# The mixing product and the FFN's first block in 1024-column blocks, with a seam by token halves

## The chip, the cores and the metric

One core of one Trainium2 chip runs the whole kernel. The metric is the device time in microseconds; the time before is the median of three runs, 1722.13 us (1721.88 to 1722.79). In the profile PE is TensorE (matmuls and transposes), DVE is VectorE, ACT is ScalarE, POOL is GpSimd, and SP issues most of the DMAs.

## The reference

One layer of a hybrid decoder block on 256 tokens of width 2048: attention and a gated recurrence run side by side, are joined by two gates, and a SwiGLU FFN follows. What matters here is its end:

```python
y = jax.nn.sigmoid(gate_a) * (attn @ w_attn_branch[layer]) + jax.nn.sigmoid(gate_r) * (r_out @ w_hgrn_branch[layer])
h = h + rmsnorm(y @ w_mix_out[layer], norm_mix_post[layer])
a = rmsnorm(h, norm_ffn_pre[layer])
gt, up = jnp.split(a @ w_ffn_gate_up[layer], [D_FF], axis=-1)
ff = (jax.nn.silu(gt) * up) @ w_ffn_down[layer]
h = h + rmsnorm(ff, norm_ffn_post[layer])
```

The mixing product is `y @ w_mix_out` (2048 x 2048). The first RMS norm needs all its columns before one column of h is known, and h's own norm is applied behind the gate and up products, as a factor per token (`r2c`).

## The kernel before

**Products.** Each float32 operand is split into a high and a low part, and a product is three matmuls: high by high, high by low, low by high. ACT makes the high part of a weight tile (`w` from `raw`), DVE the low part (`wl`). Activations are stationary, 128 tokens at a time (a *side*, or token half), and weights are streamed 512 columns at a time into PSUM banks. There are two kinds of blocks:

- An "N" block (`Block`) makes 512 output columns. Its steps, called chunks, take two 128-row slices of the depth each: 12 matmuls, into two banks.
- A wide block (`Wide`) makes two groups of 512 columns. A plain step takes a pair m of slices, for two sides and two groups: eight products, 24 matmuls, into four banks. A step marked `(m, 1)` in the block's order does the 2 x 2 x 2 of sides, groups and slices with seven products instead of eight: 21 matmuls. For that DVE and ACT form four combinations of the weights (`sum`, then `w`, `wl`) beside the parts of three of its raw groups (`dh`, `dl`), and four combinations of the activations of that pair (`pair_sums`, tiles `f`, `s`, `so`). Seven banks are open then, and `gather` and an evacuation put them together.

PSUM has two pools of four banks, `acc` and `aux`; a block's four banks are in one, its three extra ones in the other, by `flip`. Transposes take banks of either.

**What sets the order.** A list of items (chunks and steps) is walked in order. For each item `prepare(i)` splits the weights of item i + 2 and asks SP for the loads ahead (three `raw` buffers, three `w` buffers), `multiply` issues the matmuls, and then the *lanes* advance: generators for side work (norms, pair sums, transposes), which are taken one stage per step. `flush` empties such a queue on the spot. Every engine takes its instructions in the order in which this loop writes them.

**Around the change.** The items are, in order: two gate blocks, four blocks of the recurrent branch, four of the attention branch (all N blocks), four N blocks of `w_mix_out`, two N blocks for the FFN's first 512 gate and up columns, ten wide blocks (`GATE_UP`) for the others, and the down product. `evac_attn_branch` makes y, whose transposes (`turned`, tile `yT`) run into the first mixing block. `evac_mix` squares and scales each mixing block as it ends; gains and x (`gpost`, `hx`) are loaded on the ACT queue at the first. `begin_ffn` opens the FFN: six matmuls on a zero tile (`keep_warm`), the transposes of h's first pair into `hT`, and the next residuals; `more_h` brings the other pairs, one per step, and later starts the pair sums of `hT`; `second_norm` sums the squares for `r2c`. The first block's result u is transposed (`turn_act`) after the second step of the next block. Lines of before that the prediction's rows carry: L118 matmuls, L296/L297 the split of a chunk, L342/L344 of a plain step, L348 to L362 of a seven-product step, L434 to L454 pair sums, L509 and L522 transposes, L529/L533 hT, L1048 to L1086 the mixing's end, L1132 second norm, L1184/L1190 gate and u.

Of the kernel before, what the change touches and what calls it, by code (L numbers as in the profile page):

```python
# [20 lines left out]
P = 128  # L21
# [41 lines left out]
class Wide:  # L63
# [7 lines left out]
    def __init__(self, w, cols, order, xs, seven, evac, flip, prep=None, pre=None, mid=None,  # L71
                 turn=None, halves=False):
        self.w, self.cols, self.order, self.xs, self.seven = w, cols, order, xs, seven
        self.evac, self.flip, self.prep, self.pre, self.mid = evac, flip, prep, pre, mid
        self.turn, self.halves, self.post = turn, halves, None
        self.last7 = max((i for i, (m, s) in enumerate(order) if s), default=None)
        self.bank, self.open, self.rest = {}, set(), None


@with_exitstack  # L80
def tile_hybrid_block(ctx: ExitStack, tc: tile.TileContext, t, out):
# [251 lines left out]
    def split_wide(n):  # L333
# [3 lines left out]
        prep = b.prep(m, by7) if b.prep else iter(())  # L337
        next(prep, None)
        hi, lo = wslot(), p3("wl", F32R, 2048, 3)
        if not by7:  # L340
# [105 lines left out]

    x7 = {}

    def pair_sums(src, out, slot):

        for m in H7:
            f = ptile("f").rearrange("p (k t) -> p k t", k=2)
            x = src.slots[m]
            nc.vector.tensor_add(f, x[:, :, 0, :].bitcast(F32), x[:, :, 1, :].bitcast(F32))  # L454
# [318 lines left out]
    def fetch_gates():  # L773
        for j in range(2):
            gates["r", j] = nslot("gate")
            fetch(gates["r", j], ("r", j), "(b p) c -> p b c", p=P)
        for j in range(4):
            gates["a", j] = hslot("gate")
            fetch(gates["a", j], ("a", j), "(b p) c -> p b c", p=P)
# [204 lines left out]

    def evac_gate(key, slot):
        def go(banks):
            d = gates[key] = slot("gate")
            if d.ndim == 2:
                d = gates[key] = d.rearrange("p (b c) -> p b c", b=2)
            for i in range(2):  # L990
# [9 lines left out]
    def evac_rec_branch(j):  # L1000
        def go(banks):
            part[j] = nslot("part")
            for i in range(2):
# [4 lines left out]
    def evac_attn_branch(j):  # L1008
        def go(banks):
            if not yT:  # L1010
                yT.append(Split("yT", KD))
            y = nslot("y")
            for i in range(2):
                nc.vector.tensor_mul(y[:, i, :], banks[i], gates["a", j][:, i, :])
                nc.vector.tensor_add(y[:, i, :], y[:, i, :], part[j][:, i, :])
                yield
# [6 lines left out]

    def begin_mix():
        nc.scalar.preload_act_table_set("natural_log_exp_and_others")
        zss.append(small("zss"))

    def mix_loads():
        for j in range(2):
            gpost.append(fslot("gpost"))  # L1030
            nc.scalar.dma_start(
# [3 lines left out]
        for j in range(4):  # L1035
            hx[j] = fslot("hx").rearrange("p (b c) -> p b c", b=2)
            nc.scalar.dma_start(hx[j], xv[:, :, j * 512 : (j + 1) * 512])

    def evac_mix(j):
        def go(banks):  # L1040
            if j == 0:
                mix_loads()
            zg[j] = fslot("zg").rearrange("p (b c) -> p b c", b=2)
            for i in range(2):
                ps = banks[i]
                junk = ptile("junk")
                sq = zss[0][:, 4 * i + j : 4 * i + j + 1]
                nc.scalar.activation(junk, ps, AF.Square, accum_out=sq)  # L1048
                if j == 3:
                    rsqrt_mean(rzc[:, i : i + 1], sq, D, zss[1][i])  # L1050
                    residual(0, 0, 128, (i,), False)
                    residual(0, 128, 256, (i,), False)
                else:
                    post_gain(j, i, ps)
                yield
            if j == 2:
                zss.append(so_far(zss[0]))
        return go

    def post_gain(j, i, ps):  # L1060
        nc.vector.tensor_mul(
            zg[j][:, i, :], ps, gpost[j // 2][:, (j % 2) * 512 : (j % 2 + 1) * 512]
        )

    def so_far(ss):

        b = small("base")
        nc.vector.tensor_reduce(
            b[:, :2], ss.rearrange("p (b j) -> p b j", b=2)[:, :, :3], op=OP.add,
            axis=mybir.AxisListType.X,  # L1070
        )
        nc.vector.tensor_scalar(b[:, :2], b[:, :2], 1.0 / D, EPS, op0=OP.mult, op1=OP.add)
        nc.vector.tensor_scalar(b[:, 2:4], b[:, :2], -0.5, None, op0=OP.mult)
        return [(b[:, i : i + 1], b[:, 2 + i : 3 + i]) for i in range(2)]

# [13 lines left out]

    def begin_ffn():  # L1090
        keep_warm(BRIDGE)
        flush(evacs)
        hT.append(Split("hT", KD))
        high, low = transpose_in(h_t, colg[:, 16:32], hT[0], 0, True)
        for kk in range(2):
            high(kk)
            low(kk)
        residual_of(1, False)
        residual_of(2, False)

    def residual_of(m, spread=True):

        residual(m // 2, m % 2 * 256, m % 2 * 256 + 256, spread=spread)

    def mid_ffn():
        transpose_in(h_t, colg[:, 16:32], hT[0], 1)
        residual_of(3)
        lanes[0].append(second_norm())

    def more_h(c):  # L1110
        if c + 2 < KD // 2:
            transpose_in(h_t, colg[:, 16:32], hT[0], c + 2)
        if c + 4 < KD // 2:
            residual_of(c + 4)
        if c < 2:
            post_gain(3, c, blocks[last_mix].banks[c])
        if c == 5:
            end_phase1()
        if c == 6:
            lanes[1].append(  # L1120
                pair_sums(
                    hT[0], h7,
                    lambda: p3("so", F32R, 1024, 4),
                )
            )

# [22 lines left out]

    act_t, gate_t, h7 = [], {}, {}  # L1150

# [20 lines left out]

    def evac_first_gate(banks):
        g = gate_t[0] = [eslot("g") for _ in range(2)]
        src = banks
        if "r2" not in ready:
            for i in range(2):
                nc.scalar.activation(g[i], banks[i], AF.Copy)
                yield
            src = g  # L1180
            while "r2" not in ready:
                yield
        for i in range(2):
            nc.scalar.activation(g[i], src[i], AF.Silu, scale=r2c[:, i : i + 1])  # L1184
            yield

    def evac_first_up(banks):
        u = [eslot("u") for _ in range(2)]
        for i in range(2):
            nc.vector.scalar_tensor_tensor(  # L1190
                out=u[i], in0=banks[i], scalar=r2c[:, i : i + 1], in1=gate_t[0][i],
                op0=OP.mult, op1=OP.mult,
            )
        turns.append(u)
        yield

# [127 lines left out]
    def begin_wides():  # L1324
        flush(evacs)
        flush(lanes[1])

    early = [
        ("g", "g", COL_GR, 512),
        (("a", 0), ("a", 1), COL_GA, 512),  # L1330
        (("a", 2), ("a", 3), COL_GA + 1024, 512),
        (("r", 0), ("r", 1), COL_GB, 512),
    ]
# [23 lines left out]
    for j in range(2, 4):  # L1357
        add("N", w_in, KD, COL_GB + 512 * j, xT, evac_gate(("r", j), fslot))
    for j in range(4):
        add("N", t["w_hgrn_branch"][0], 8, 512 * j, lambda k: recT[0](k), evac_rec_branch(j),  # L1360
            pre=begin_branches if j == 0 else None)
    for j in range(4):
        add("N", t["w_attn_branch"][0], 8, 512 * j, lambda k: attnT[0](k), evac_attn_branch(j),
            pre=flush_lanes if j == 0 else None)
    for j in range(4):
        add("N", t["w_mix_out"][0], KD, 512 * j, lambda k: yT[0].after(turns)(k), evac_mix(j),
            pre=begin_mix if j == 0 else None)
    last_mix = len(blocks) - 1
    w = t["w_ffn_gate_up"][0]
    add("N", w, KD, 0, lambda k: hT[0](k), evac_first_gate,  # L1370
        pre=begin_ffn, mid=mid_ffn, post=more_h)
    add("N", w, KD, FF, lambda k: hT[0](k), evac_first_up)
    for j in range(1, 11):
# [20 lines left out]
    for i in range(len(items)):  # L1394
# [7 lines left out]
        if not wide and n in items_pre:  # L1402
            items_pre[n]()
        if not (wide and b.mid):
            prepare(i)
# [82 lines left out]
```

## Time and profile before

| | |
|---|---|
| median of three runs | 1722.13 us |
| profiled execution | 1722.56 us, span 1720.8 us |
| granted clock of TensorE, mean | 0.998 |
| busy: PE, DVE, ACT | 1703.5, 1358.7, 898.7 us |
| mixing product, first to last matmul | 914.79 to 1003.30 us |
| FFN's first block | up to 1053.66 us, where the first `GATE_UP` step starts |

A row of a timeline gives the start, the duration, the engine, the line, the operation, its tiles and how many instructions it merges; in brackets stands the idle time before it and what ended that. A row of the windows gives, after its length, the busy time and number of instructions of PE, weight loads, DVE, ACT and POOL, then the clock that TensorE was granted, the DMA share and GB/s. A row of the groups gives busy time and the mean of one in ns, and the idle time of its engine ahead of it. Matmuls are pipelined: one of 512 columns is shown with 0.39 us, while the next starts sooner.

### The profile page before, as it was taken

The numbers are of one execution on the slowest core, as the hardware profiler recorded it, in microseconds if no ns is written. First come the engines' busy times: TensorE is split into PE (matmuls) and PEld (weight loads), VectorE is DVE, ScalarE is ACT, GpSimd is POOL, SyncE is SP. The second block draws the span as 40 slices with busy tenths as digits, with TensorE's granted clock in tenths as the row PEclk, the third lists the DMA queues.
The fourth block names the chain that finished last, engine by engine and source line by source line (L and its number), as shares of the span: only waits on it lengthen the run. The fifth ranks groups of instructions, "written<-read, shape, count | busy, mean of one in ns | idle before, by whom it ended". The sixth has DMA issues, their size and how long they took to land.

```text
span 1720.8 us, 21495 instructions
## 1 busy us (share of the span) xinstructions
PE 1703.5 (99%) x8356; PEld 1429.9 (83%) x8357; DVE 1358.7 (79%) x1486; ACT 898.7 (52%) x1016; POOL 6.5 (0%) x16
## 2 busy tenths in 40 slices
PE   9999999999999999999999999999999999999997
PEld 7788888888888888888888878888888888888886
DVE  6888888866787877774566578888888888898997
ACT  6455555544434434445444466555555555665663
POOL 0000000000000000000000000000000000000000
PEclk9999999999999999999999999999999999999999
DMA  8466666655544545475456745555556555656663
GB/s 289 162 237 241 232 221 220 229 189 194 172 159 160 197 135 163 155 254 187 159 172 204 245 163 196 196 197 200 201 202 202 201 202 197 221 191 215 201 197 114
DMA packets 207189, 338.48 MB, mean 197 GB/s; under 512 B 10688, under 2 KB 77424, under 8 KB 207088
## 3 DMA queue, kind: packets, MB, share of 16 engines
q1 hardware_dynamic: 201360, 325.71, 56.9%
q10 hardware_dynamic: 5728, 11.41, 1.8%
q8 instruction: 65, 1.06, 0.3%
q14 instruction: 36, 0.29, 0.1%
HBM read 328.69 MB, written 8.39 MB: 196 GB/s over the span
## 4 chain that ended last, share of the span: by engine, by line
PE 89%; DVE 6%; issue 2%; ACT 2%; DMA 1%; ACTq 0%; DVEq 0%; SPq 0%
PE acc L118 61%; PE aux L118 26%; DVE wl L344 1%; DVE wl L360 1%; DVE dl L362 1%; DVE sum L348 1%; ACT w L356 1%; ACT w L342 0%; PE aux L522 0%; DVE sum L355 0%; DVE sum L354 0%; PE aux L840 0%; DMA gpost<-in_norm_mix_post 0%; DMA raw<-in_w_ffn_gate_up 0%; PE aux L1166 0%
## 5 line engine op out<-in xcount | busy, mean ns | idle before, releaser
L297 DVE TENSOR_TENSOR w<-raw,w 128x1024 fp32r<-128x1024 f32 x224 | 274.1, 1224 | 194.9 <-ACT w L296 193.1
L296 ACT ACTIVATE w<-raw 128x1024 fp32r<-128x1024 f32 x224 | 237.0, 1058 | 292.8 <-PE acc L118 263.0
L118 PE MATMUL acc<-xT,w 128*128 128x256 f32 (+1 forms) x2048 | 366.6, 338 | 0.0
L118 PEld LDWEIGHTS acc<-xT,w 128*128 128x128 f32 x2048 | 311.6, 188 | 44.0
L344 DVE TENSOR_TENSOR wl<-raw,w 128x2048 fp32r<-128x2048 f32 (+1 forms) x131 | 284.1, 2173 | 48.7 <-ACT w L342 46.4
L342 ACT ACTIVATE w<-raw 128x2048 fp32r<-128x2048 f32 (+1 forms) x131 | 237.7, 1819 | 103.1 <-PE acc L118 34.9
L360 DVE TENSOR_TENSOR wl<-sum,w 128x2048 fp32r<-128x2048 f32 x63 | 144.3, 2291 | 57.4 <-ACT w L356 57.4
L118 PE MATMUL acc<-w,hT 128*128 128x512 f32 x622 | 183.1, 391 | 0.3 <-ACT hT L529 0.3
L118 PE MATMUL acc<-w,xT 128*128 128x512 f32 x578 | 169.4, 392 | 0.0
L353 ACT ACTIVATE w<-sum 128x1024 fp32r<-128x1024 f32 x63 | 67.0, 1063 | 195.6 <-DVE sum L348 195.6
L118 PE MATMUL aux<-w,hT 128*128 128x512 f32 x430 | 137.3, 389 | 0.0
L118 PEld LDWEIGHTS acc<-w,hT 128*128 128x128 f32 x622 | 116.1, 188 | 24.5 <-ACT hT L529 0.5
L118 PEld LDWEIGHTS acc<-w,xT 128*128 128x128 f32 x578 | 108.1, 188 | 22.2
L362 DVE TENSOR_TENSOR dl<-raw,dh 128x1536 fp32r<-128x1536 f32 x63 | 110.4, 1752 | 0.0
L118 PE MATMUL aux<-w,xT 128*128 128x512 f32 x344 | 109.8, 389 | 0.0
L359 ACT ACTIVATE dh<-raw 128x1536 fp32r<-128x1536 f32 x63 | 93.2, 1479 | 6.6 <-PE aux L118 3.4
L118 PEld LDWEIGHTS aux<-w,hT 128*128 128x128 f32 x430 | 80.7, 188 | 16.8
L118 PE MATMUL acc<-w,yT 128*128 128x512 f32 x384 | 88.2, 390 | 0.1
L118 PEld LDWEIGHTS acc<-w,yT 128*128 128x128 f32 x384 | 71.8, 188 | 15.3 <-DVE w L297 0.5
L118 PE MATMUL acc<-w,a 128*128 128x512 f32 x268 | 83.7, 389 | 0.5 <-DVE e L1200 0.5
L118 PE MATMUL aux<-w,a 128*128 128x512 f32 x268 | 83.7, 389 | 0.0
L118 PE MATMUL aux<-wl,hT 128*128 128x512 f32 x215 | 83.6, 389 | 0.0
(262 smaller groups left out, 2624.2 us busy)
## 6 DMA issues: line engine op xcount, KB each, us to landing
raw<-in_w_in SPq DMA_DIRECT2D x270, 512.0 KB, 4.6
raw<-in_w_ffn_gate_up SPq DMA_DIRECT2D x176, 512.0 KB, 4.6
raw<-in_w_ffn_down SPq DMA_DIRECT2D x88, 512.0 KB, 4.8
raw<-in_w_mix_out SPq DMA_DIRECT2D x32, 512.0 KB, 4.9
raw<-in_w_hgrn_branch SPq DMA_DIRECT2D x16, 512.0 KB, 4.6
raw<-in_w_attn_branch SPq DMA_DIRECT2D x16, 512.0 KB, 4.5
waits<-e ACTq DMA_DIRECT2D x24, 256.0 KB, 2.6
v<-waits SPq DMA_DIRECT2D x6, 512.0 KB, 7.0
```

The lines of the kernel that those rows point to most:

```text
L118: nc.tensor.matmul(ps, lhsT, rhs, start=start, stop=stop, skip_group_check=True)
L296: nc.scalar.activation(wh, raw, AF.Copy)
L297: nc.vector.tensor_sub(wl, raw, wh.bitcast(F32))
L342: nc.scalar.activation(hi[:, c], raw[:, c], AF.Copy)
L344: nc.vector.tensor_sub(lo[:, c], raw[:, c], hi[:, c].bitcast(F32))
L348: nc.vector.tensor_sub(s[:, :1024].rearrange("p (a c) -> p a c", a=2), raw[:, 512:1536].rearrange("p (a c) -> p a c", a=2), raw[:, None, : ...
L353: nc.scalar.activation(hi[:, :1024], s[:, :1024], AF.Copy)
L356: nc.scalar.activation(hi[:, 1024:], s[:, 1024:], AF.Copy)
L359: nc.scalar.activation(dhi, d, AF.Copy)
L360: nc.vector.tensor_sub(lo, s, hi.bitcast(F32))
L362: nc.vector.tensor_sub(dlo, d, dhi.bitcast(F32))
```

## The change

- The mixing product becomes two wide blocks of 1024 columns, in orders `MIX`, with the pairs 0 and 1 by seven products: four of 16 steps. Their activation sums come from `pair_sums` on `yT` (`more_y`), and the blocks are evacuated like the down product (`mix_sum`, `mix_square`, `mix_gain`).
- The FFN's first block becomes one wide block of plain steps over the first 512 gate and up columns.
- The last two mixing steps and the first three FFN steps are written out in `mix_to_ffn` by token halves: both steps' matmuls of one side and one group, then the other; the first half's norm, residual and transposes (`turn_side`) stand between them. One of the FFN steps keeps its split weights in buffers of its own (`spare`, `Joined`). `begin_ffn` with its six matmuls on the zero tile is gone.
- The pair sums of `hT` start at step 5 of the eight and `second_norm` at step 4; `begin_wides` empties both lanes before the first `GATE_UP` step.
- The pools of the first phase are closed in the first attention-branch block (`make_room`), y is written over the attention gate, and gains, x and the branch parts use other buffers. Of the eight gate blocks, the two computed last are now those of the attention branch instead of the recurrent one.

```diff
+MIX = [
+    [(3, 0), (4, 0), (0, 1), (5, 0), (1, 1), (2, 0), (6, 0), (7, 0)],
+    [(2, 0), (3, 0), (0, 1), (4, 0), (1, 1), (5, 0), (6, 0), (7, 0)],
+]
...
+        if (b, i) == spare:
+            hi = p3("spare", F32R, 2048, 1, "sum")
+            lo = Joined(p3("spare", F32R, 1536, 1, "dh"), p3("spare", F32R, 512, 1, "dl"))
+            nc.scalar.activation(hi, raw, AF.Copy)
+            for c in (slice(0, 1536), slice(1536, 2048)):
+                nc.vector.tensor_sub(lo[:, c], raw[:, c], hi[:, c].bitcast(F32))
...
+    def mix_to_ffn(i):
...
+        prepare(i)
+        mix(0, 0)
+        base = third(0)
+        mix(0, 1)
+        norm(0, base)
+        residual(0, 0, 256, (0,), False)
+        prepare(i + 1)
+        mix(1, 0)
+        base = third(1)
+        residual(0, 256, 512, (0,), False)
+        mix(1, 1, (0,))
+        hT.append(Split("hT", KD))
+        turn_side(0, 0)
+        mix(1, 1, (1,))
+        norm(1, base)
+        turn_side(1, 0)
+        residual_of(2, (0,), False)
+        prepare(i + 2)
+        ffn(0, 0)
+        turn_side(2, 0)
+        residual(0, 0, 256, (1,), False)
+        ffn(1, 0)
+        turn_side(0, 1)
...
     def more_h(c):
...
+        if c + 1 < KD // 2:
+            transpose_in(h_t, colg[:, 16:32], hT[0], c + 1)
...
+        if c == 4:
+            residual_of(6)
+            residual_of(7)
+            lanes[0].append(second_norm())
         if c == 5:
...
+            lanes[1].append(pair_sums(hT[0], h7, lambda: p3("so", F32R, 1024, 4)))
...
     def begin_wides():
-        flush(evacs)
-        flush(lanes[1])
+        for lane in lanes:
+            flush(lane)
...
+    for j in range(2):
+        last_mix = len(wides)
+        add_wide_block(t["w_mix_out"][0], (1024 * j, 1024 * j + 512), MIX[j],
+                       lambda k: yT[0].after(turns)(k), lambda m: y7[m], evac_mix, j == 0,
+                       pre=begin_mix if j == 0 else None)
...
+    add_wide_block(w, (0, FF), PLAIN, lambda k: hT[0](k), None, evac_first, True, mid=more_h)
```

How the order moves on the engines, at three places. On PE at the seam, before: the last zero-tile matmul, the transposes of h's first 256 columns and the first FFN matmuls (`h` is the residual, `hT` its transpose, `w` a split weight).

```order
L118 LDWEIGHTS warm
L118 MATMUL aux_7945<-warm 128x512
L522 MATMUL aux_7986<-ident,h_7963 128x128 x2
L522 MATMUL aux_7989<-ident,h_7963 128x128 x2
L118 MATMUL acc_8007<-w_7912,hT_7978 128x512 x6
L522 MATMUL aux_8015<-ident,h_7963 128x128 x4
L118 MATMUL acc_8008<-w_7912,hT_7978 128x512 x6
```

On PE at the seam, now: the end of the mixing's last bank (on `yT`), two pairs of transposes of the first token half, and the first FFN matmuls.

```order
L1110 MATMUL aux_8017<-ident,h_7971 128x128 x2
L135 MATMUL aux_7728<-w_7889,yT_7114 128x512
L135 MATMUL aux_7728<-wl_7890,yT_7114 128x512
L135 MATMUL aux_7728<-w_7889,yT_7114 128x512 x2
L135 MATMUL aux_7728<-wl_7890,yT_7114 128x512
L135 MATMUL aux_7728<-w_7889,yT_7114 128x512
L1110 MATMUL aux_8041<-ident,h_7971 128x128 x2
L135 MATMUL acc_8057<-w_7920,hT_8009 128x512
```

The zero-tile matmuls are gone, and six matmuls of the mixing stand between the two pairs of transposes. On DVE the rows that lead to the second of these pairs are now: the first half's factor (`rzc`) and h, the spare split, the next bank's sum and gain, and h's second 256 columns.

```order
L153 SCALAR_TENSOR_TENSOR rzc<-a_7965,y_7964 128x1
L1097 SCALAR_TENSOR_TENSOR h_7971<-zg_7737,rzc,hx_7386 128x256
L361 TENSOR_TENSOR spare_7974<-raw_7856,spare_7973 128x1536
L361 TENSOR_TENSOR spare_7975<-raw_7856,spare_7973 128x512
L1063 TENSOR_TENSOR e_7883<-aux_7721,e_7883 128x512
L1072 TENSOR_TENSOR zg_7942<-e_7883,gpost_7384 128x512
L1339 TENSOR_REDUCE base_7998<-zss_7381 128x1
L1342 TENSOR_SCALAR base_7998<-base_7998 128x1
L1343 TENSOR_SCALAR base_7998<-base_7998 128x1
L1097 SCALAR_TENSOR_TENSOR h_7971<-zg_7737,rzc,hx_7386 128x256
```

Before, at this place DVE had the factor and two pieces of h per side, and no split:

```order
L132 SCALAR_TENSOR_TENSOR a_7957<-y_7956,v_7955 128x1
L136 SCALAR_TENSOR_TENSOR rzc<-a_7957,y_7956 128x1
L1086 SCALAR_TENSOR_TENSOR h_7963<-zg_7538,rzc,hx_7530 128x128 x2
L130 TENSOR_SCALAR v_7968<-zss_7352,base_7860 128x1
L132 SCALAR_TENSOR_TENSOR a_7970<-y_7969,v_7968 128x1
L136 SCALAR_TENSOR_TENSOR rzc<-a_7970,y_7969 128x1
L1086 SCALAR_TENSOR_TENSOR h_7963<-zg_7538,rzc,hx_7530 128x128 x2
```

The split of a weight tile and the sum of another bank have come between the factor and the columns that PE transposes. On DVE at the first `GATE_UP` steps, before: the two u, the last pair sum, and the first seven-product split.

```order
L1190 SCALAR_TENSOR_TENSOR u_8421<-acc_8264,r2c,g_8278 128x512
L1190 SCALAR_TENSOR_TENSOR u_8422<-acc_8265,r2c,g_8279 128x512
L441 TENSOR_TENSOR so_8396<-s_8416,so_8396 128x512
L348 TENSOR_TENSOR sum_8429<-raw_8343 128x1024
L354 TENSOR_TENSOR sum_8429<-raw_8343,sum_8429 128x512
L355 TENSOR_TENSOR sum_8429<-raw_8343,sum_8429 128x512
L360 TENSOR_TENSOR wl_8428<-sum_8429,w_8427 128x2048
L362 TENSOR_TENSOR dl_8436<-raw_8343,dh_8435 128x1536
```

The same place on DVE now:

```order
L466 TENSOR_TENSOR so_8456<-s_8457,so_8456 128x512
L373 TENSOR_TENSOR sum_8466<-raw_8318 128x1024
L379 TENSOR_TENSOR sum_8466<-raw_8318,sum_8466 128x512
L380 TENSOR_TENSOR sum_8466<-raw_8318,sum_8466 128x512
L385 TENSOR_TENSOR wl_8465<-sum_8466,w_8464 128x2048
L387 TENSOR_TENSOR dl_8473<-raw_8318,dh_8472 128x1536
L1256 SCALAR_TENSOR_TENSOR u_8448<-acc_8064,r2c,g_8446 128x512
L1256 SCALAR_TENSOR_TENSOR u_8449<-acc_8138,r2c,g_8447 128x512
```

The two u have moved from ahead of the split to behind it.

More of the change, by code (lines that the diff above doesn't have):

```diff
@@ L1035, in mix_loads @@
         for j in range(4):
-            hx[j] = fslot("hx").rearrange("p (b c) -> p b c", b=2)
+            hx[j] = rslot("hx").bitcast(F32).rearrange("p (b c) -> p b c", b=2)
             nc.scalar.dma_start(hx[j], xv[:, :, j * 512 : (j + 1) * 512])
[L1039 to L1058, printed above, removed]
@@ L1065, in so_far @@
[L1065 to L1074, printed above, removed]
+            zg[j][:, i, :], b.rest[i, j % 2],
```

201 lines of the change are left out of this document (127 added, 74 removed).

## Prediction

> **What bounds the kernel now.** I read the page's busy shares first, then a table of windows around the change, then the timelines of PE, ACT and DVE there.
>
> ```profile
> PE 1703.5 (99%) x8356; PEld 1429.9 (83%) x8357; DVE 1358.7 (79%) x1486; ACT 898.7 (52%) x1016; POOL 6.5 (0%) x16
> ```
> ```profile
> 915.00:1003.00 88.00, 87.95 (x392) 72.38 (x391) 47.44 (x48) 40.87 (x51) 0.00 (x0) 1.00 0.68 227
> 1003.00:1006.50 3.50, 2.42 (x12) 1.02 (x11) 2.33 (x11) 2.04 (x8) 0.00 (x0) 1.00 0.63 193
> ```
> ```profile
> 902.60 0.60 PE L509 MATMUL aux<-ident,y 128*128 128x128 f32 x4
> ...
> 914.79 8.43 PE L118 MATMUL acc<-w,yT 128*128 128x512 f32 x36
> ...
> 926.63 76.82 PE L118 MATMUL acc<-w,yT 128*128 128x512 f32 x336
> 1003.30 1.47 PE L118 MATMUL aux<-warm 128*128 128x512 bf16 x5
> 1004.60 0.27 PE L522 MATMUL aux<-ident,h 128*128 128x128 f32 x1
> ...
> 1006.52 1.71 PE L118 MATMUL acc<-w,hT 128*128 128x512 f32 x6 [0.30 <-ACT hT L529]
> ...
> 1013.22 0.60 PE L522 MATMUL aux<-ident,h 128*128 128x128 f32 x4
> 1013.57 2.99 PE L118 MATMUL acc<-w,hT 128*128 128x512 f32 x12
> ...
> 1026.01 0.60 PE L522 MATMUL aux<-ident,h 128*128 128x128 f32 x4
> ...
> 1053.66 0.39 PE L118 MATMUL aux<-w,hT 128*128 128x512 f32 x1
> ...
> 1070.19 0.39 PE L118 MATMUL aux<-w,hT 128*128 128x512 f32 x1
> ...
> 1075.63 0.39 PE L118 MATMUL acc<-w,so 128*128 128x512 f32 x1
> ```
>
> TensorE is busy all the time. In the mixing product (914.79 to 1003.30) it never waits to speak of, and DVE and ACT are busy for half of it. Only the 3.5 us of the seam to the FFN show a hole. So what the change removes on PE counts in full, and so does each new wait on PE; the question is whether DVE and ACT, which get more work in shorter bursts, still keep ahead. Two prices on PE: a plain eight-product step is 24 matmuls from 1070.19 to 1075.63, 0.227 us each; four transposes cost 0.35 (1013.22 to 1013.57).
>
> **What is saved on PE.** Four of 16 mixing steps go from 24 matmuls to 21: 12 x 0.227 = 2.7 us. The six warm-up matmuls go: 1003.30 to 1004.60, 1.3 us. From there to the first FFN matmul are 1.92 us, of which four transposes are 0.35: 1.6 us of waiting go. Together 5.6 us. The FFN block keeps its 192 matmuls, and the transposes keep their number.
>
> **What it costs: six waits.** The orders of the change put elementwise work in front of what PE wants next. I lay the rows of before end to end in the new order. Durations:
>
> ```profile
> L342 ACT ACTIVATE w<-raw 128x2048 fp32r<-128x2048 f32 x117 | 223.4, 1910 | 99.8 <-PE acc L118 34.9 <-PE aux L118 24.7 <-issue 23.9
> ```
> ```profile
> L297 DVE TENSOR_TENSOR w<-raw,w 128x1024 fp32r<-128x1024 f32 x224 | 274.1, 1224 | 194.9 <-ACT w L296 193.1
> L1015 DVE TENSOR_TENSOR y<-y,part 128x512 f32<-128x512 f32 x8 | 5.5, 692 | 0.3
> L1086 DVE SCALAR_TENSOR_TENSOR h<-zg,rzc,hx 128x256 f32<-128x256 f32 x9 | 4.8, 563 | 0.0
> ```
> ```profile
> 1033.00 0.15 DVE L602 TENSOR_REDUCE s<-ss 128x2 f32<-128x8 f32 x1
> ...
> 1034.14 0.16 DVE L136 SCALAR_TENSOR_TENSOR r2c<-a,y 128x2 f32<-128x2 f32 x1
> ...
> 1052.69 0.68 DVE L454 TENSOR_TENSOR f<-hT 128x512 f32<-128x512 f32 x1
> 1053.29 2.28 DVE L344 TENSOR_TENSOR wl<-raw,w 128x2048 fp32r<-128x2048 f32 x1
> 1055.49 0.28 DVE L434 SCALAR_TENSOR_TENSOR s<-f 128x128 f32<-128x128 f32 x1
> ...
> 1056.42 1.41 DVE L1190 SCALAR_TENSOR_TENSOR u<-acc,r2c,g 128x512 f32<-128x512 f32 x2
> 1057.74 0.68 DVE L441 TENSOR_TENSOR so<-s,so 128x512 fp32r<-128x512 f32 x1
> 1058.34 1.22 DVE L348 TENSOR_TENSOR sum<-raw 128x1024 f32<-128x1024 f32 x1
> ...
> 1066.02 2.28 DVE L344 TENSOR_TENSOR wl<-raw,w 128x2048 fp32r<-128x2048 f32 x1
> ```
> ```profile
> 1003.49 0.60 ACT L1048 ACTIVATE junk<-acc 128x512 f32<-128x512 f32 x1
> ...
> 1004.54 0.20 ACT L129 ACTIVATE y<-y 128x1 f32<-128x1 f32 x1
> ...
> 1026.64 0.84 ACT L529 ACTIVATE hT<-aux,colg 128x256 fp32r<-128x256 f32 x2 [0.81 <-PE aux L522]
> 1027.37 0.63 ACT L1132 ACTIVATE junk<-h 128x512 f32<-128x512 f32 x1
> ...
> 1027.98 0.63 ACT L1132 ACTIVATE junk<-h 128x512 f32<-128x512 f32 x1
> ...
> 1034.69 1.28 ACT L1184 ACT_TABLE_LOAD   x1
> 1035.98 0.69 ACT L1184 ACTIVATE g<-acc,r2c 128x512 f32<-128x512 f32 x1
> ```
>
> Neighbours overlap by 0.08 on DVE and 0.10 on ACT (1053.29 with 2.28 is followed at 1055.49). So on DVE a wide split takes 2.2 us, a chunk's split 1.14, a 512-column operation 0.6 (0.7 where the next needs its result), the four pieces of a pair's sums 1.0 (1055.49 to 1056.42 and a little), and the whole split of a seven-product step, from its first sum to the next instruction, 7.7 (1058.34 to 1066.02, with one round through ACT). A 512-column operation on ACT is 0.6 (1027.37 to 1027.98). A one-column operation I estimate at 0.17, and two of 128 columns at 0.4, from the r2 chain and the pieces. PE takes its instructions in order, so behind each wait stand all later matmuls, and nothing after it gives the time back.
>
> *Wait 1, the third bank of the first mixing step.* A wide block takes four acc banks where two sufficed, so its third waits for the last attention block's first product. Count from the transposes that stand at 902.60. They and ACT's copy take 1.2; then DVE has five 512-column operations (three yT, an f, a so) 3.0, two chunk splits 2.3, two products with their sums 2.6, two wide splits 4.4, eight pieces 2.0, the awaited product 0.7: 16.2. PE needs 914.79 - 902.60 = 12.2 and 12 matmuls, 2.7: 14.9. Wait 1.3.
>
> *Wait 2, the third product of the first seven-product step,* needs the aux bank that DVE's put of the last y frees, and this put stands behind two splits. From the awaited product on: sum, product, sum 2.0, the seven-product split 7.7, so 0.6, wide split 2.2, put 0.7: 13.2. PE has 42 matmuls and eight transposes, 10.2. Wait 3.0.
>
> *Wait 3, the transposes of h's second 256 columns at the seam.* From the release of the slot for the first FFN split (ACT starts): 1.9; DVE split 2.2; sum and gain 1.4; three small operations 0.5; the next sum 0.7; square, Ln and Exp 1.25 (1003.49 to 1004.74); ACT's spare split 1.9 and DVE's, in two pieces, 2.3; sum and gain 1.4; three small 0.5; h 0.56: 14.6. PE has 48 matmuls and two transposes, 11.1. Wait 3.5. The six matmuls that are the last cover between the token halves are far too short for the spare split, which stands in between.
>
> *Waits 4 and 5, the next two pairs of transposes,* each behind 12 matmuls and a pair, 2.9. For the first: two small hT 0.4, sum 0.6, square to Exp 1.25, two small 0.4, hT 0.4, h 0.56: 3.7 with hand-overs. For the second the ACT split still has 0.9 to run, then DVE's 2.2, hT 0.4, h 0.5: 4.0. Waits 0.8 and 1.1.
>
> *Wait 6, the transposes of u after the second step of the next block.* Before, pair sums and the second norm were spread over two blocks of 16 chunk steps; now they start at steps 4 and 5 of eight, and what is left is emptied in front of the next split, and u stands behind that split. From the last transposes (1026.01 of before): to ACT's copies 0.63, these 0.73; a split 1.8, a square 0.6, so 0.5, two squares 1.2, a split 1.9 (7.4 so far); DVE's split 2.2; f 0.6; r2's chain 1.3 (1033.00 to 1034.30); the table load 1.29; two Silu 1.2; so on ACT 0.65; on DVE so 0.6, f 0.7, pieces 1.0; so on ACT 0.66 and on DVE 0.6; the seven-product split 7.7; two u 1.3: 27.2. PE has 84 matmuls and four transposes, 19.4. Wait 7.8. Without u the wait would not go: the seven-product split of that step, which PE wants next, ends at 25.9 of this count.
>
> The row of the table load is 1.28, and the next row starts 1.29 behind it. [...]
>
> Sum of the waits: 1.3 + 3.0 + 3.5 + 1.9 + 7.8 = 17.5. Less 5.6: +11.9.
>
> **What a long wait does to the clock.**
>
> ```profile
> 1710.99 0.39 PE L118 MATMUL aux<-w,a 128*128 128x512 f32 x1
> ```
> ```profile
> 1713.00:1714.00 1.00, 0.00 (x0) 0.00 (x0) 0.58 (x3) 0.49 (x2) 0.00 (x0) 0.92 0.00 0
> 1714.00:1715.00 1.00, 0.00 (x0) 0.00 (x0) 1.00 (x3) 0.00 (x0) 0.00 (x0) 0.50 0.00 0
> ```
> ```profile
> 1.19 3.59 PE L118 MATMUL aux<-warm 128*128 128x512 bf16 x8 [1.19 <-DVE warm L142]
> ```
>
> The last matmul ends at 1711.38, and a mean of 0.92 in 1713 to 1714 puts the fall of the granted clock to 0.50 at 1713.84: 2.5 us of idle PE. Waits 3 and 6 are longer; wait 2 is at the edge. How long the clock stays down once matmuls run, before doesn't show in mid-kernel. At the start matmuls take 0.45 (3.59 for eight), twice the 0.227, until about 7 us: 6 us, so at most 3.0 us are lost per fall, and at least nothing. I take the middle, 1.5, no row being nearer to one end, for two falls: +3.0. [...]
>
> **Moved at no cost.** The six loads of gains and x move from the middle of the mixing to its start.
>
> ```profile
> ACT junk L1048 <- issue: 3.0, 1, 3.0
> ```
>
> Their 3.0 us of issuing on the ACT queue now stand, with the table load, between two splits, when ACT waits for DVE's sums of the first seven-product split anyway; without that cover up to 3.0 more. The SP queue keeps its order and number of loads. POOL's additions for the second token half each come a step ahead of their transposes. The gates only swap places.
>
> Sum: 1722.13 + 11.9 + 3.0 = 1737.0 us. The profiled execution was 1722.56 (span 1720.8), 0.43 above the median; its terms carry over.
>
> **Rivals.**
> - *The clock doesn't fall, or is back at once.* For it: the two falls are priced from the ends of the kernel alone. 1722.1 + 11.9 = 1734.
> - *Wait 6 is hidden,* if DVE and ACT empty the pair sums and the norm while PE still does the first block: it takes that their chain starts 7.8 us earlier. Against: its start hangs on PE's own last transposes. 9.7 - 5.6, one fall 1.5: 1727.7.
> - *Faster:* the elementwise queues keep a lead of two steps (2 x 5.44 us) through the mixing and the seam, so that no burst reaches PE; it ends faster once the waits sum to less than 5.6, a third of mine. For it: DVE is busy 47.44 of 88 us in the mixing. Against: a split can't start before PE frees its slot, so a lead isn't stored. 1722.1 - 5.6 = 1716.5.
> - *DVE stays behind after the waits* in the seven-product steps that follow each: one more wait like 2 or 3, and a third fall, about +5: 1742.
>
> **Chances.** Forecast 0.48, clock unmoved 0.24, wait 6 hidden 0.12, faster 0.08, further behind 0.08. The range 1728 to 1741 leaves out the faster case and most of the last. A difference under 0.2% (3.4 us) can't be told from none: faster 0.08, same 0.03, slower 0.89.
>
> **What would show it.** On PE, idle ahead of the transposes of h released by DVE h, and ahead of those of u, near 7.8; two short ones at the mixing's start released by DVE; the granted clock at 0.50 behind them; no warm-up. It is wrong if the waits of PE there sum to less than 12 us, or if the seven-product steps save less than 2.7.

## The result and the profile after

The changed kernel takes 1736.97 us (median of four runs, 1736.04 to 1738.36), the kernel before 1722.41 on the same chip: a ratio of 1.0085 with an interval of 1.0072 to 1.0098. Predicted were 1737.0 us. The profiled execution is one of 1736.95 us with a span of 1735.1.

First the line of the page with the busy times, the one that opens the prediction.

```profile
PE 1703.4 (98%) x8339; PEld 1430.1 (82%) x8339; DVE 1387.4 (80%) x1512; ACT 905.3 (52%) x1012; POOL 10.9 (1%) x18
```

PE is busy as long as before (1703.5 us) although the mixing has 12 matmuls less and the warm-up is gone (about 4.0 us): some matmuls take longer, those that run while the granted clock is at 0.50: they start 0.43 us apart there (72.22 to 75.21), and 0.23 at 1.00 (1082.82 to 1085.99). The span has grown by 14.3 us, and all of it is time in which PE waits. Where, two windows of the changed kernel show (length, then busy time of PE, weight loads, DVE, ACT and POOL, the clock, DMA):

```profile
915.00:1000.00 85.00, 81.60 (x365) 66.91 (x364) 70.19 (x63) 42.55 (x41) 0.00 (x0) 1.00 0.69 236
1000.00:1100.00 100.00, 87.01 (x389) 70.51 (x388) 72.75 (x103) 56.88 (x87) 8.18 (x7) 0.95 0.43 147
```

In the mixing PE was idle for 0.05 of 88 us before and now for 3.4 of 85, and DVE's share of the time has gone from 54% to 83%. In the hundred microseconds of the seam and the FFN's first block 13 us are idle, and the granted clock has a mean of 0.95. The timeline of PE in the changed kernel, only the rows with an idle time in brackets and, ahead of the last of them, the FFN block's last transposes:

```profile
919.75 0.50 PE L135 MATMUL acc<-w,yT 128*128 128x512 f32 x1 [1.03 <-DVE gate L1037]
...
932.89 0.50 PE L135 MATMUL aux<-w,so 128*128 128x512 f32 x1 [2.37 <-DVE yT L515]
...
1009.15 0.44 PE L1110 MATMUL aux<-ident,h 128*128 128x128 f32 x2 [3.61 <-DVE h L1097]
...
1013.14 0.44 PE L1110 MATMUL aux<-ident,h 128*128 128x128 f32 x2 [0.78 <-DVE h L1097]
...
1017.15 0.44 PE L1110 MATMUL aux<-ident,h 128*128 128x128 f32 x2 [0.80 <-DVE h L1097]
...
1049.88 0.60 PE L547 MATMUL aux<-ident,h 128*128 128x128 f32 x4
...
1077.22 2.32 PE L1241 MATMUL acc<-ident,u 128*128 128x128 f32 x8 [7.69 <-DVE u L1256]
```

These are the six waits of the prediction, in their places and with the releasers it named; they sum to 16.3 us. What stands ahead of the longest, the timeline of DVE shows:

```profile
1060.37 0.15 DVE L627 TENSOR_REDUCE s<-ss 128x2 f32<-128x8 f32 x1
...
1061.51 0.16 DVE L153 SCALAR_TENSOR_TENSOR r2c<-a,y 128x2 f32<-128x2 f32 x1
...
1064.94 0.69 DVE L466 TENSOR_TENSOR so<-s,so 128x512 fp32r<-128x512 f32 x1 [2.33 <-ACT so L465]
...
1068.66 1.22 DVE L373 TENSOR_TENSOR sum<-raw 128x1024 f32<-128x1024 f32 x1
...
1076.33 1.40 DVE L1256 SCALAR_TENSOR_TENSOR u<-acc,r2c,g 128x512 f32<-128x512 f32 x2
```

From the sum of squares (1060.37) to u (1076.33) DVE does the chain to r2c, what is left of two pairs' sums, and the whole seven-product split from 1068.66 on, with pauses for ACT in between, the longest of 2.33 us; PE's last matmul of the step before ended at 1069.54 (the third window of the next table: 0.83 from 1068.71 on).

The clock, in windows of the changed kernel that are 3.41 us long (why this length, the experiments tell):

```profile
1003.85:1007.27 3.42, 1.70 (x9) 1.08 (x7) 2.85 (x3) 0.54 (x1) 0.00 (x0) 1.00 0.00 0
1007.27:1010.68 3.41, 1.53 (x8) 1.31 (x9) 2.78 (x9) 1.67 (x5) 0.00 (x0) 1.00 0.82 267
1068.71:1072.12 3.41, 0.83 (x4) 0.36 (x2) 2.55 (x4) 1.81 (x2) 0.00 (x0) 1.00 0.01 2
1072.12:1075.53 3.41, 0.00 (x0) 0.00 (x0) 3.08 (x2) 3.41 (x3) 0.00 (x0) 0.50 0.00 0
...
1078.95:1082.36 3.41, 3.41 (x11) 2.73 (x10) 3.34 (x4) 2.03 (x3) 0.00 (x0) 0.50 0.89 303
1082.36:1085.77 3.41, 3.41 (x17) 2.82 (x16) 2.28 (x2) 1.06 (x1) 0.00 (x0) 1.00 0.55 211
```

It is at 0.50 from 1072.12 to 1082.36. PE resumes at 1077.22, so 5.1 us of its work go at 0.50. By that share I estimate 2.6 us lost (by the 0.43 and 0.23 us between matmuls 2.4). In the 3.61 us of wait 3 (1005.55 to 1009.15) it did not fall. It did fall once far ahead of the change, in the first phase, at two waits of 1.47 and 0.90 us (from 68.0 and 70.9):

```profile
68.61:72.03 3.42, 1.66 (x6) 1.09 (x7) 3.39 (x4) 2.81 (x3) 0.00 (x0) 1.00 0.00 0
72.03:75.44 3.41, 3.41 (x9) 2.63 (x9) 3.38 (x4) 0.00 (x0) 0.00 (x0) 0.50 0.87 306
```

That is, by the same share, 1.7 us more lost, and at no place that the change touches: the kernel before has the same two waits (1.47 and 0.88 from 66.8 and 69.7), and in its profiled execution the clock stayed at 1.00 there. The two stretches at 0.50, an estimated 4.3 us together, make up for the 4.0 us of work saved, which is why PE's busy time is as before.

### The profile page after: what moved, and what is told of

It is laid out like the page before. It is cut to its first block, busy times and chain, and to the rows that moved or that the text cites. A ratio compares the mean times of both kernels' runs of the same rounds, so it can differ in the third digit from the quotient of the medians.

```text
span 1735.1 us, 21461 instructions
## 1 busy us (share of the span) xinstructions
PE 1703.4 (98%) x8339; PEld 1430.1 (82%) x8339; DVE 1387.4 (80%) x1512; ACT 905.3 (52%) x1012; POOL 10.9 (1%) x18
## 4 chain that ended last, share of the span: by engine, by line
PE 86%; DVE 8%; ACT 3%; issue 3%; DMA 0%; ACTq 0%; SPq 0%; DVEq 0%
PE acc L135 56%; PE aux L135 28%; DVE wl L369 2%; DVE wl L385 1%; ACT w L367 1%; DVE sum L373 1%; DVE dl L387 1%; ACT w L381 1%; DVE sum L380 0%; DVE sum L379 0%; PE aux L865 0%; DMA x<-in_x 0%; PE aux L547 0%; PE acc L1241 0%; PE aux L1241 0%
## 5 line engine op out<-in xcount | busy, mean ns | idle before, releaser
L369 DVE TENSOR_TENSOR wl<-raw,w 128x2048 fp32r<-128x2048 f32 (+1 forms) x150 | 327.8, 2189 | 64.9 <-ACT w L367 64.1
L314 DVE TENSOR_TENSOR w<-raw,w 128x1024 fp32r<-128x1024 f32 x176 | 215.5, 1224 | 152.8 <-ACT w L313 151.1
L367 ACT ACTIVATE w<-raw 128x2048 fp32r<-128x2048 f32 (+1 forms) x150 | 274.2, 1831 | 118.6 <-PE acc L135 48.0
L313 ACT ACTIVATE w<-raw 128x1024 fp32r<-128x1024 f32 x176 | 186.3, 1059 | 246.6 <-PE acc L135 220.1
L385 DVE TENSOR_TENSOR wl<-sum,w 128x2048 fp32r<-128x2048 f32 x67 | 153.5, 2292 | 62.0 <-ACT w L381 62.0
L135 PE MATMUL acc<-w,hT 128*128 128x512 f32 x542 | 173.9, 391 | 0.0
L135 PEld LDWEIGHTS acc<-w,hT 128*128 128x128 f32 x542 | 101.7, 188 | 21.1
L387 DVE TENSOR_TENSOR dl<-raw,dh 128x1536 fp32r<-128x1536 f32 x67 | 117.4, 1753 | 1.5 <-ACT dh L384 1.4
L135 PE MATMUL acc<-wl,hT 128*128 128x512 f32 x271 | 105.5, 389 | 0.0
L373 DVE TENSOR_TENSOR sum<-raw 128x1024 f32<-128x1024 f32 x67 | 81.7, 1220 | 0.4 <-DMA raw<-in_w_ffn_down 0.4
```

Of the source, the lines that this page charges most:

```text
L135: nc.tensor.matmul(ps, lhsT, rhs, start=start, stop=stop, skip_group_check=True)
L313: nc.scalar.activation(wh, raw, AF.Copy)
L314: nc.vector.tensor_sub(wl, raw, wh.bitcast(F32))
L367: nc.scalar.activation(hi[:, c], raw[:, c], AF.Copy)
L369: nc.vector.tensor_sub(lo[:, c], raw[:, c], hi[:, c].bitcast(F32))
L373: nc.vector.tensor_sub(s[:, :1024].rearrange("p (a c) -> p a c", a=2), raw[:, 512:1536].rearrange("p (a c) -> p a c", a=2), raw[:, None, : ...
```

## The experiments

Every kernel here is the changed kernel with the edit shown. Times are medians beside that of the kernel before on the same chip, and the difference between them is what is compared (the changed kernel: +14.6). Each profile shows one execution of its kernel; what is said of the clock is read from that one.

**fill_u_wait: is the clock part of the price?**

```diff
         if wide and c == b.turn:
             flush(evacs)
+            if b is wides[last_mix + 2]:
+                ps = acc_bank()
+                for _ in range(28):
+                    mm(ps, warm[:, :P], warm, True, True)
             turn_act(turns.popleft())
```

> 28 matmuls on a zero tile (28 x 0.227 = 6.4 us) are put on PE into the 7.7 us wait ahead of the transposes of u; nothing else moves. Theory (the clock falls in that wait and costs half of the 5.1 us in which matmuls then run at 0.42): about 1.3 us of waiting stay in front of u, no 0.50 in the clock there, and the time is 1734.4 us, 2.6 less than the changed kernel; by the 1.5 that the prediction priced per fall, 1735.5. Rival (the fall costs nothing, since DVE and ACT bound what follows): 1737.0.

Measured: 1735.51 us (1734.44 to 1736.14) beside 1722.49, +13.0. The timeline of PE and one window of this kernel:

```profile
1067.40 6.22 PE L135 MATMUL acc<-warm 128*128 128x512 bf16 x28
1075.24 0.30 PE L1241 MATMUL acc<-ident,u 128*128 128x128 f32 x1 [1.62 <-DVE u L1256]
```
```profile
1073.63:1077.04 3.41, 1.53 (x10) 1.33 (x11) 3.41 (x4) 0.65 (x2) 0.00 (x0) 1.00 0.38 98
1077.04:1080.45 3.41, 3.41 (x9) 2.64 (x9) 3.34 (x4) 1.49 (x2) 0.00 (x0) 0.50 0.86 294
```

The gain of 1.5 goes to the clock, so the rival (no cost) is out, though only just by these runs: the changed kernel's begin at 1736.04, where these end at 1736.14 (fill_three_waits, further down, is clearer). The expectation that no 0.50 would be left is wrong: after only 1.9 us of waiting (1.6 and 0.3) the clock fell at 1077.04 and was back at 1080.45, 3.41 us later. The length of the idle stretch alone does not tell the cases apart: at the 3.61 us of wait 3 in the changed kernel it did not fall. In the changed kernel's profile the fall and the rise at wait 6 are 10.24 us apart, 3.00 times 3.413, and the fall at its end (1730.91) comes 193.0 such periods after that first one; here the end's fall comes 190.0 periods after the one at 1077.04. So in these traces the falls and rises lie on borders 3.413 us apart. In the period ahead of the fall PE was busy for 1.53 us of 3.41 here, and for 0.83 in the changed kernel.

**spread_sums: is wait 6 a backlog that can be spread?**

```diff
-        if c == 5:
+        if c == 3:
             lanes[1].append(pair_sums(hT[0], h7, lambda: p3("so", F32R, 1024, 4)))
...
     def begin_wides():
-        for lane in lanes:
-            flush(lane)
+        flush(lanes[0])
```

> The pair sums of hT start at step 3 instead of 5, and only the lane of the second norm is emptied ahead of the first GATE_UP step. Theory (wait 6 is the backlog of pair sums and norm that is emptied in front of the seven-product split): the wait ahead of u falls from 7.7 to about 1.7 us, the clock stays at 1.00, and the time is 1737.0 - 5.9 - 2.6 = 1728.5 us. Rival (DVE is saturated, so the wait comes back in the seven-product steps that follow): u's wait falls, others of together 4 to 6 us appear between 1080 and 1110, time 1733 to 1737.

Measured: 1728.65 us (1726.97 to 1730.73) beside 1722.49, +6.2. Its waits of PE between 890 and 1120 us (total, times, longest), and two pairs of windows:

```profile
PE aux L1110 <- DVE h L1097: 3.9, 2, 3.6
PE aux L135 <- DVE yT L515: 2.4, 1, 2.4
PE acc L1241 <- DVE u L1256: 1.8, 2, 1.6
PE acc L135 <- DVE gate L1037: 1.0, 1, 1.0
```
```profile
927.55:930.96 3.41, 1.28 (x6) 0.73 (x4) 3.41 (x4) 0.85 (x2) 0.00 (x0) 1.00 0.82 257
930.96:934.37 3.41, 3.18 (x8) 2.51 (x9) 3.28 (x5) 1.08 (x2) 0.00 (x0) 0.50 1.03 369
1006.05:1009.47 3.42, 0.55 (x4) 0.51 (x5) 3.25 (x10) 1.24 (x4) 0.00 (x0) 1.00 0.50 130
1009.47:1012.88 3.41, 3.41 (x10) 2.67 (x9) 2.11 (x7) 2.80 (x7) 0.00 (x0) 0.50 0.48 182
```

Wait 6 goes from 7.7 to 1.8, and nothing comes back behind it: the rival of a saturated DVE falls. The price is met within 0.2 us, though not in the way expected: the clock fell twice, at waits 2 and 3, which are as long as in the changed kernel's profile, where it did not. The borders lie elsewhere in this execution: the same wait 3 left 1.70 and 1.53 us of busy PE in two periods there, and 0.55 in one here. That would also explain why these five runs spread over 3.8 us; fill_three_waits tests it. (Behind the fall wait 4 is gone: PE at 0.50 arrives later.)

**late_sevens and plain_mix: what do the seven-product steps bring?** late_sevens:

```diff
-    [(3, 0), (4, 0), (0, 1), (5, 0), (1, 1), (2, 0), (6, 0), (7, 0)],
+    [(2, 0), (3, 0), (4, 0), (5, 0), (0, 1), (6, 0), (1, 1), (7, 0)],
```

> The first mixing block's order becomes (2,0) (3,0) (4,0) (5,0) (0,1) (6,0) (1,1) (7,0): its first seven-product step comes fifth instead of third. Theory (wait 2 is that step's aux bank, freed by DVE's put of yT behind the seven-product split and the next one): the 2.4 us wait goes and none takes its place, 1737.0 - 2.6 = 1734.4 us. Rival (DVE has no room for a seven-product split anywhere in this block): the wait moves to the fifth step with 2 us or more, 1736.5 to 1737.5.

plain_mix:

```diff
-MIX = [
...
+MIX = [PLAIN, PLAIN]
...
-        f = b.rest[i, j % 2]
-        nc.vector.tensor_add(f, b.bank[i, j % 2], f)
+        if b.rest is None:
+            b.rest = {}
+        f = b.rest[i, j % 2] = p3("e", F32, 512, 6)
+        nc.vector.tensor_copy(f, b.bank[i, j % 2])
```

> Both mixing blocks are made of eight plain steps (no seven-product step; the bank is copied where it was added to the gathered part). Theory (four seven-product steps save 12 matmuls, 2.7 us, and cost wait 2, 2.4 us): 2.7 more of matmuls, wait 2 gone, 1737.0 to 1737.5 us, so that the seven-product steps bring nothing on balance here. Rival (wait 2 hangs on the transposes of y alone and stays): 1739.7 us. Second rival (the seven-product steps also cause part of the other waits through DVE): under 1735.5.

Measured: late_sevens 1732.74 us (1731.41 to 1733.75) beside 1722.49, +10.3; plain_mix 1736.21 (1735.52 to 1736.49), +13.7. The waits of late_sevens between 890 and 1120 us, then the one that plain_mix has between 900 and 1000:

```profile
PE acc L1241 <- DVE u L1256: 7.7, 1, 7.7
PE aux L1110 <- DVE h L1097: 5.2, 3, 3.6
PE acc L135 <- DVE gate L1037: 1.0, 1, 1.0
```
```profile
PE acc L132 <- DVE gate L1034: 1.0, 1, 1.0
```

In both, wait 2 is gone, so it belongs to the early place of the first seven-product step. As the change puts them, the four steps bring nothing against plain ones (+14.6 and +13.7); with the first block's two put two places later, the four are worth 3.5 us against plain ones. late_sevens is 1.7 better than expected: with wait 2 also goes a place where the clock can fall, which fits but is not shown apart.

**fill_three_waits: the clock's whole share.** Three waits are filled a little short of their length: 9 zero-tile matmuls in the bank of `p6` ahead of the first mixing step by seven products, 32 instead of 28 ahead of u, and

```diff
+        keep_warm(13)
         turn_side(1, 0)
         residual_of(2, (0,), False)
```

> Zero-tile matmuls fill three waits of the changed kernel without moving anything else: 9 (2.0 us) ahead of the first seven-product step's sums, 13 (2.9 us) ahead of the second pair of transposes of h, 32 (7.3 us) ahead of the transposes of u; each is a little shorter than its wait. Theory (the granted clock is set every 3.41 us by TensorE's busy share in the 3.41 us before, and where those borders lie differs from execution to execution, so that waits 2, 3 and 6 each cost nothing, or one or two such periods at half rate): no 0.50 between 900 and 1120 us, 1737.0 - 3.0 = 1734.0 us, and five runs that lie within about 1.0 us as those of the kernel before do, where spread_sums had 3.8. Rival (the clock costs only what it lost in wait 6, 2.6, and fill_u_wait's 1.5 is all that can be had back): 1735.5. Rival (the spread has another cause): runs over 2 us apart.

Measured: 1733.47 us (1732.80 to 1733.83) beside 1722.05, +11.4. No 0.50 stands between 860 us and the fall at the kernel's end (1726), and the runs lie within 1.0 us. So the clock costs the changed kernel 14.56 - 11.42 = 3.1 us between the medians, in which falls in the first phase, like the one in its profile, may have a share. The rest, 11.4, is PE's waiting less what was saved, 16.3 - 5.6 = 10.7, with 0.7 left open.

**no_spare_low, h_before_spare, seam_only: what are the seam's waits made of?** no_spare_low:

```diff
-            lo = Joined(p3("spare", F32R, 1536, 1, "dh"), p3("spare", F32R, 512, 1, "dl"))
...
-            for c in (slice(0, 1536), slice(1536, 2048)):
-                nc.vector.tensor_sub(lo[:, c], raw[:, c], hi[:, c].bitcast(F32))
-            steps[n][3] = hi, lo
+            steps[n][3] = hi, hi
```

> The low part of the spare step's weights is left out (its matmuls read the high part in its place), which takes 2.36 us of DVE out of the seam. Theory (waits 3 to 5 are DVE's backlog at the seam, conserved in order): waits 3 to 5 fall from 5.2 to about 2.8 us, time 1734.4 us less what the clock gains, 1733 to 1734.5. Rival (the chain sum, square, Ln, Exp, h of each half bounds the seam, DVE's load doesn't): waits 3 to 5 stay over 4.5, time 1736.5.

h_before_spare:

```diff
         residual(0, 0, 256, (0,), False)
+        residual(0, 256, 512, (0,), False)
         prepare(i + 1)
         mix(1, 0)
         base = third(1)
-        residual(0, 256, 512, (0,), False)
```

> h's second 256 columns are formed ahead of the spare split instead of behind it and the next bank's sum. Theory (the waits at the seam are a backlog, so putting one piece first moves the wait to the next piece): wait 3 falls from 3.6 to under 0.5, but a wait of 2.5 to 3 appears at the mixing bank that ends the half or at the next transposes; sum of the seam's waits 4.9 to 5.8, time 1736.5 us. Rival, as the prediction put it (the spare split in between is what the transposes wait for): the sum falls by the 3.6 of wait 3, time 1733.4.

seam_only:

```diff
         def norm(s, base):
             mix_sum(3, s, b)
             mix_square(3, s, b)
+            base = so_far_of(zss[0], s)
...
         prepare(i)
+        prepare(i + 1)
...
         residual(0, 0, 256, (0,), False)
-        prepare(i + 1)
...
         residual_of(2, (0,), False)
+        residual(0, 0, 256, (1,), False)
         prepare(i + 2)
         ffn(0, 0)
         turn_side(2, 0)
-        residual(0, 0, 256, (1,), False)
```

(`third` no longer forms the partial sum.)

> The changed kernel with the three edits at the seam alone (the spare split right behind the first one, the norm's partial sum behind the next bank's sum, the second half's first residual ahead of the next split); waits 1, 2 and 6 stay. Theory (the seam's waits fall from 5.2 to 2.4 as in combined, by order alone, since they are made of hand-overs between ACT and DVE as well as of DVE's load): 1737.0 - 2.8 = 1734.2 us. Rival (conserved backlog, as h_before_spare showed; in combined the seam gained from the earlier splits of late_sevens): 1736 to 1737.

Measured: no_spare_low 1732.15 us (1731.92 to 1734.26) beside 1722.05, +10.1; h_before_spare 1736.26 (1734.46 to 1737.21), +14.2; seam_only 1731.61 (1731.23 to 1732.12) beside 1722.29, +9.3. PE's waits at the seam, in this order:

```profile
PE aux L1107 <- DVE h L1094: 2.1, 3, 0.8
```
```profile
PE acc L135 <- ACT hT L1116: 2.7, 1, 2.7
PE aux L1110 <- DVE h L1097: 2.0, 2, 1.2
```
```profile
PE aux L1110 <- DVE h L1097: 2.4, 2, 1.4
```

no_spare_low leaves out the low part of one step's weights, 2.4 us of DVE work, and the seam waits 3.1 less; wait 3 alone goes from 3.6 to 0.5. With h's piece moved alone wait 3 goes, but 2.7 us come back at the first FFN matmul: 4.7 in all against 5.2. ACT and DVE in h_before_spare show why:

```profile
1007.85 0.63 ACT L1067 ACTIVATE junk<-e 128x512 f32<-128x512 f32 x1 [3.03 <-DVE e L1063]
...
1008.47 0.60 ACT L1116 ACTIVATE hT<-aux,colg 128x128 fp32r<-128x128 f32 x2
```
```profile
1004.85 2.36 DVE L361 TENSOR_TENSOR spare<-raw,spare 128x1536 fp32r<-128x1536 f32 x2 [0.47 <-ACT spare L359]
1007.13 0.69 DVE L1063 TENSOR_TENSOR e<-aux,e 128x512 f32<-128x512 f32 x1
```

ACT takes the hT of that matmul behind the next bank's square, and the square waits for a sum that DVE takes behind the spare split. So the same split holds up both h and, by way of ACT's queue, hT. Both runs fit a backlog. But seam_only has the same work in another order and waits 2.4, so the backlog isn't conserved: part of the 5.2 was DVE standing still for ACT, as in the changed kernel's timeline of DVE:

```profile
1002.06 0.21 DVE L147 TENSOR_SCALAR v<-zss,base 128x1 f32<-128x1 f32 x1 [0.85 <-ACT junk L1067]
...
1004.42 2.36 DVE L361 TENSOR_TENSOR spare<-raw,spare 128x1536 fp32r<-128x1536 f32 x2 [0.87 <-ACT spare L359]
```

With the partial sum behind the next bank's sum, and both splits ahead of the sums, such pauses have work in them. Which of the three edits did how much was not measured apart. Its time is 2.4 better than the waits alone would make it (2.8 of the 5.2 from +14.6 to +9.3), which goes with fewer long waits at which the clock can fall; it isn't shown run by run.

**combined and combined_filled.** combined is late_sevens, spread_sums and seam_only in one.

> spread_sums and late_sevens together, and at the seam: the spare split right behind the first one, the norm's partial sum behind the next bank's sum instead of ahead of it, and the second half's first residual ahead of the next split. Theory: wait 2 goes (2.4), u's wait falls to 1.9 (5.9), the seam's waits from 5.2 to about 2.9, and no wait is left that lowers the clock (2.6 or more): 1737.0 - 2.4 - 5.9 - 2.3 - 2.6 = 1723.8 us, some 1 us slower to level with the kernel before. Rival (the seam's backlog is conserved here too and a fall stays): 1727.

Measured: 1721.69 us (1720.97 to 1723.93) beside 1722.05, a ratio of 1.0001 (0.9992 to 1.0010). Its waits from 890 to 1120 us, and two windows:

```profile
PE aux L1110 <- DVE h L1097: 2.4, 2, 1.4
PE acc L1241 <- DVE u L1256: 1.8, 2, 1.5
PE acc L135 <- DVE gate L1037: 1.0, 1, 1.0
```
```profile
1062.19:1065.60 3.41, 1.64 (x11) 1.33 (x11) 3.41 (x5) 1.16 (x3) 0.00 (x0) 1.00 0.39 101
1065.60:1069.01 3.41, 3.41 (x9) 2.66 (x9) 3.35 (x3) 1.17 (x2) 0.00 (x0) 0.50 0.75 237
```

5.2 us of waits are left against 5.6 saved: -0.4, as measured (which leaves next to nothing for the clock in the median run). It is level with the kernel before, and so gives back the whole of the change's loss. One fall was still there in the profiled execution (1722.97 us), so I filled these waits too:

```diff
+        keep_warm(4)
         turn_side(0, 0)
...
         ffn(0, 0)
+        keep_warm(3)
         turn_side(2, 0)
```

and 5 matmuls ahead of u, as in fill_u_wait.

> combined, with zero-tile matmuls in its three longest waits: 4 (0.9 us) ahead of the first and 3 (0.7 us) ahead of the third pair of transposes of h, 5 (1.1 us) ahead of the transposes of u. Theory (combined's runs between 1722.4 and 1723.9 us are those in which a 3.41 us period at u's wait was too idle, those near 1721.2 had none): no 0.50 between 900 and 1120 us, all runs within about 1 us of 1721.2, 0.8 us under the kernel before's 1722.05, which five rounds may just tell apart. Rival (the two groups of runs have another cause): runs up to 1723.9 again, median 1721.7.

Measured: 1721.84 us (1721.10 to 1722.76) beside 1722.29, a ratio of 0.9997 (0.9988 to 1.0006). No fall is left between 860 us and the one at the kernel's end (1714.1), and no run lies above 1722.8, but the median hasn't moved: the 1721.2 expected, 0.8 us under the kernel before, is not there (it is 0.45 under), and nothing here tells this kernel from the one before.

## Why the prediction was right, step by step

- **The waits.** Predicted and measured: 1.3 and 1.03; 3.0 and 2.37; 3.5 and 3.61; 0.8 and 0.78; 1.1 and 0.80; 7.8 and 7.69; the sum 17.5 and 16.3. For wait 6 the count from the last transposes (1049.88) to those of u is 27.3 us and PE's cover 19.7, where 27.2 and 19.4 were predicted. Laying the rows of before end to end in the new order worked. Only the third is longer than predicted; the largest miss is 0.6, at wait 2.
- **The savings of 5.6.** Not seen alone, but two sums close on it: fill_three_waits (10.7 by waits and savings, 11.4 measured) and combined (-0.4 and -0.4). Both show only the balance of waits and savings, to 0.7 us.
- **The cause of wait 6** held: spread_sums took 5.9 of 7.7 away. **That of wait 2** held (late_sevens, plain_mix). **That of wait 3** held, and was not the whole of it: the spare split does stand in between (no_spare_low), but taking h out from behind it gains only 0.5 in waits, because the sum, square and hT behind it wait as well; the seam's waits hang on the whole order of sums, squares and splits on two engines.
- **The clock: right in size, wrong in detail.** 1.5 for each of two falls made +3.0; measured are 3.1. But "2.5 us of idle PE" as what makes it fall is the step that failed. It was read from one fall at the end of the kernel, which shows how long PE had been idle there and not how long it has to be. In the profiled execution wait 3 (3.61 us) lowered nothing, and of the six waits wait 6 alone cost clock, an estimated 2.6; in spread_sums waits 2 and 3, of the same length, cost an estimated 1.6 and 1.7. So by these two profiles the 3.1 hangs on where the borders lie in a run, and two errors (a fall at wait 3 that this execution does not have, too low a price for the one at wait 6) cancelled. The fall at 72 us is in no term of the sum. The agreement with 1737.0 to 0.1 us (+14.9 predicted on 1722.13, +14.6 measured on 1722.41) is luck to that degree.
- **The loads at no cost** held. ACT's timeline in the changed kernel:

```profile
916.89 4.47 ACTq L1059 DMA_DIRECT2D hx<-in_x  x4
922.98 1.06 ACT L378 ACTIVATE w<-sum 128x1024 fp32r<-128x1024 f32 x1 [5.06 <-DVE sum L373]
```

  The issuing was over at 921.36, and DVE's sum released ACT only at 922.98, 1.6 us later.
- **The table load** took 1.28 us (1061.75) and the next row starts 1.30 later, where before had 1.28 and 1.29.
- **The rivals.** "Clock doesn't fall" is the case that fill_three_waits makes: 1733.5, where 1734 was given for it; the changed kernel is not it. "Wait 6 is hidden" and "DVE stays behind" didn't happen: PE waits 7.69 in the one place, and behind it nothing above 0.5 until the end. "Faster" needed waits under 5.6; combined, with 5.2, shows that this bound was right, and that even then there is little to win. The range began at 1728, 0.3 above the 1727.7 given for "wait 6 is hidden", so it left out that case too, which its sentence does not say.

## What to carry to other kernels

Sixteen microseconds of waits came from a DVE that was busy for 73 to 83% of the time there and not for all of it: what counts is how much side work is emptied in front of the one result that the bounding engine takes next, so start such work steps earlier, empty only the queue whose result is due, and put a hand-over's waiting time to use with another split or sum. Saved matmuls (here 2.7 us) are worth nothing while the split that pays for them sits close ahead of a bank that is waited for; try them later in the block before giving them up. And price a hole on TensorE at its length plus a clock term that differs from run to run (the five runs of spread_sums, whose profile has falls at two waits, spread over 3.8 us, those of fill_three_waits over 1.0): compare medians of several runs, and try filling holes that can't be closed (worth 3.1 us in fill_three_waits, nothing in combined_filled, whose holes were short).

## What the hardware showed that I had not expected

The clock's changes lie on a grid: in each of the nine profiles that show one ahead of the kernel's end, the times between falls and rises are whole multiples of 3.4133 us (1 to 486 periods, to 0.02), and the grid's place differs from execution to execution (a fall at 1072.12 in the changed kernel and at 1077.04 in fill_u_wait, 1.44 periods apart). What goes with it is the busy time of PE in one period: the clock fell behind periods with up to 1.66 us of busy rows of 3.41 (the changed kernel, from 68.61) and stayed up behind 1.52 (late_sevens, from 1003.95) and more. Between these two the rows do not separate the cases: 1.64 stands ahead of a fall in combined (from 1062.19) and of none in seam_only (from 929.05). They draw short transposes too long (four, at 1049.88, are shown with 0.60, and the next matmul starts 0.35 later). The changed kernel's fall at 72.03 stands behind two waits, of 1.47 and 0.90 us, with work between them. So the clock fell at a wait of 1.9 us (1.6 and 0.3 taken together) in fill_u_wait and at one of 2.4 in spread_sums, and it did not fall at waits of 2.4 and 3.6 in the changed kernel. Once down, it came back at the border behind a period that was busy for 3.18 us (spread_sums, from 930.96) or more, and not behind one of 2.18 (plain_mix, from 1006.68). So PE ran at 0.50 for 3.2 to 3.4 us (spread_sums, fill_u_wait) or, where a half idle period came first, 5.1 us (the changed kernel); by the granted share such a fall costs half of that, an estimated 1.6 to 2.6 us.
